# q and k products made with tokens on partitions ahead of the gMLP mixing, split and kept in DRAM with v

## The chip, the core and the metric

The kernel runs on one core of a Trainium2 chip: TensorE (PE) multiplies, VectorE (DVE), ScalarE (ACT) and GpSimd (POOL) do the rest, and SyncE (SP) issues every DMA on one queue. Times are device microseconds of one execution.

## What is computed

One layer of a decoder trunk on 1024 tokens of width 1024, all in float32:

```python
h = rmsnorm(x, norm_g)
gate_pre, a_in, a_z, b_uv, b_z, q, k, v, c_z, f_pre = split_columns(h @ w_in)
y_a = (silu(layernorm(conv31(glu(a_in)))) * silu(a_z)) @ w_a      # 512 channels
y_b = (u * (tril(w_s) @ rmsnorm(v_b) + b_s) * silu(b_z)) @ w_b    # 128-token chunks
q, k = rmsnorm(q per head), rmsnorm(k per head)                   # 8 heads of 64
s = q @ k.T / 8 + c_query - c_key, causal                         # c = cumsum(log_sigmoid(f))
y_c = ((softmax(s) @ v) * silu(c_z)) @ w_c
x = x + (sum_i sigmoid(gate_pre_i + b_gate_i) * y_i) @ w_out
```

## The kernel before

Every float32 product is made of three products of a type that TensorE takes at full rate: each operand is split into hi (rounded) and lo (the rest), and hi*hi + hi*lo + lo*hi is summed in PSUM. `h` is kept in SBUF transposed, as `h_hi` and `h_lo`, features on partitions.

Most products go through `gemm_steps` (L152): a slab of 128 weight columns is stationary, 512 tokens of `h` move, and one step of the generator is one of eight pieces of the contraction, three matmuls. A slab is 2 halves x 8 = 16 steps. `slab` (L137) loads the raw weights in two DMAs; ACT makes `w_hi` (L147), POOL `w_lo` (L148, in some stages DVE). TensorE's order is the order in which the program is written; the other engines' order is made by a scheduler with priorities. Generators wait in `queue`, and `fill(n)` (L173) issues n steps of it, so that products stand between the pieces of attention, whose data come from other engines.

The stages in order of time:

1. x is normalized and transposed, and v (with the forget gate) is made for 8 tiles of 128 tokens: `prod` (L371), tokens on partitions. v is copied to `vp` in SBUF (L391).
2. `glu_steps` (L225), four times: the conv's inputs, stored to DRAM. The conv itself is 248 taps on DVE (L265, L268), spread over the stages by `pace` (L277).
3. `mixing` (L534), 8 tiles: the gMLP's v with h stationary and 512 weight columns moving (L540, `tv`), its norm (L543, `rsqrt`), hi and lo (L547, L548) and the product with the mixing weights (L557). Steps from `queue` stand between: q and k of the first two heads (`qk_steps`, L187) and three gate products.
4. Attention, eight heads, each in ten places (L736): `turned` transposes scores (L669), `weigh` multiplies with v (L689), `score` (L624) makes a block row (products L646 and L647, bias and row minimum on DVE L650, Exp on ACT L655, scaling on POOL L658). Between them `fill` takes steps of `queue`: q and k of the next pair of heads, gate products whose raw result goes to DRAM (`gate_pre`), and the four u products.
5. The products of the z paths (`gated`), merges by branch, beside them branch A's layer norm (`norm_steps`, L842), and the output projection (L956).

q and k of a pair of heads come with features on partitions. Their mean of squares per head is a product with a matrix of blocks (`ones_hd`, L206 and L207), after which ACT, POOL and DVE normalize `qn`. For each head `ready` (L704) then calls `stack` (L597), which writes the stacked hi and lo of q and k: two casts on ACT, one on DVE, and four subtractions on POOL (L608, L611; for head 0 two of them on DVE); and `head_v` (L614), one cast on ACT and one subtraction on POOL.

Of the kernel before, what the change touches and what calls it, by code (L numbers as in the profile page):

```python
# [33 lines left out]
def trunk_kernel(ctx, tc, x, norm_g, w_in, b_gate, conv_w, conv_b, conv_norm_g, conv_norm_b,  # L34
# [152 lines left out]
    def qk_steps(c0, gcol, res):  # L187
        w = slab(w2, KC, c0)
        qn = prep.tile([P, S], F32, name="qn", bufs=2)
        res.append(qn)  # L190

        def evac(hf, ps, ts):
            raw = qn[:, ts]
            sq = prep.tile([P, HALF], F32, name="sq")
            hi = prep.tile([P, HALF], F32R, name="sqhi")
            lo = prep.tile([P, HALF], F32R, name="sqlo")
            nc.scalar.copy(raw, ps)
            nc.scalar.activation(hi, ps, AF.Square)
            nc.scalar.activation(sq, ps, AF.Square)
            nc.vector.tensor_tensor(lo, sq, f32(hi), op=ALU.subtract)  # L200

            def stat():
                y0 = prep.tile([P, HALF], F32, name="y0")
                s2 = prep.tile([P, HALF], F32, name="s2")
                st = stp.tile([P, HALF], F32, name="st", tag="st")
                nc.tensor.matmul(st, lhsT=ones_hd, rhs=hi, start=True, stop=False)  # L206
                nc.tensor.matmul(st, lhsT=ones_hd, rhs=lo, start=False, stop=True)  # L207
                rsqrt(None, st, y0, s2, s2)
                nc.gpsimd.tensor_tensor(raw, raw, y0, op=ALU.mult)
                nc.vector.scalar_tensor_tensor(raw, raw, vec[:, gcol:gcol + 1], s2,  # L210
                                               op0=ALU.mult, op1=ALU.mult)

            later.append([7, stat])

        yield from gemm_steps(w, hT, evac)


# [83 lines left out]

    with ExitStack() as ph:
# [39 lines left out]
        junk = prep.tile([P, D], F32, name="junk", tag="qn", bufs=2)  # L342
# [113 lines left out]
        qk0 = []  # L456
        queue += [glu_steps(j) for j in range(JA)]
# [556 lines left out]
```

## Time and profile before

| | us |
|---|---|
| median of 3 runs (1088.1 to 1088.93) | 1088.33 |
| the profiled execution | 1089.2 |
| its span, from the first to the last instruction | 1087.2 |
| PE busy, share of the span | 1068.3, 98% |
| DVE | 672.0, 62% |
| ACT | 472.2, 43% |
| POOL | 314.7, 29% |

Busy times are unions of the instructions' intervals. Matmuls overlap in their records, so the pace of PE is read from how many start in a stretch, not from how long one is. The granted clock is the share of full speed that TensorE was given: 1.00 is 2.4 GHz, 0.50 is 1.2 GHz.

### The profile page before, as it was taken

The numbers are of one execution on the slowest core, as the hardware profiler recorded it, in microseconds if no ns is written. First come the engines' busy times: TensorE is split into PE (matmuls) and PEld (weight loads), VectorE is DVE, ScalarE is ACT, GpSimd is POOL, SyncE is SP. The second block draws the span as 40 slices with busy tenths as digits, with TensorE's granted clock in tenths as the row PEclk, the third lists the DMA queues.
The fourth block names the chain that finished last, engine by engine and source line by source line (L and its number), as shares of the span: only waits on it lengthen the run. The fifth ranks groups of instructions, "written<-read, shape, count | busy, mean of one in ns | idle before, by whom it ended". The sixth has DMA issues, their size and how long they took to land.

```text
span 1087.2 us, 14430 instructions
## 1 busy us (share of the span) xinstructions
PE 1068.3 (98%) x5256; PEld 896.8 (82%) x5256; DVE 672.0 (62%) x1232; ACT 472.2 (43%) x885; POOL 314.7 (29%) x297
## 2 busy tenths in 40 slices
PE   8999999999999899999999999999999999999998
PEld 7988888888878788888887888878887788888887
DVE  7547788868687758885788553325653455387111
ACT  6431124424466344654574443336766433365000
POOL 0022321214665556575657554300100000000000
PEclk9999999999999899999999999999999999999999
DMA  8213321113222232133222222122345234372321
GB/s 301 82 30 99 98 68 40 30 59 104 81 59 68 76 102 67 48 99 88 59 59 86 80 87 88 39 78 65 99 137 173 70 124 127 98 244 95 107 97 58
DMA packets 109442, 99.72 MB, mean 92 GB/s; under 512 B 7405, under 2 KB 82197, under 8 KB 109372
## 3 DMA queue, kind: packets, MB, share of 16 engines
q1 hardware_dynamic: 109372, 98.81, 29.7%
q8 instruction: 41, 0.67, 0.2%
q14 instruction: 29, 0.24, 0.1%
HBM read 76.21 MB, written 22.58 MB: 91 GB/s over the span
## 4 chain that ended last, share of the span: by engine, by line
PE 78%; DVE 9%; ACT 5%; DMA 4%; issue 2%; POOL 1%; SPq 0%; DVEq 0%; ACTq 0%; POOLq 0%
PE ps L160 54%; PE ops L956 8%; PE tv L540 4%; DVE acc L268 3%; PE o L689 3%; PE tpp L669 2%; PE pa L385 1%; PE pb L386 1%; PE s L646 1%; PE s L647 1%; DMA gt<-gpre 1%; PE pm L557 1%; DVE sqlo L200 1%; DVE plo L675 1%; DMA raw<-in_w_in_dram 1%
## 5 line engine op out<-in xcount | busy, mean ns | idle before, releaser
L160 PE MATMUL ps<-h_hi,w_hi 128*128 128x512 f32 x896 | 358.1, 400 | 2.4 <-ACT w_hi L147 1.6
L160 PE MATMUL ps<-h_hi,w_lo 128*128 128x512 f32 x896 | 351.6, 392 | 4.1 <-POOL w_lo L148 3.3
L160 PE MATMUL ps<-h_lo,w_hi 128*128 128x512 f32 x896 | 350.1, 391 | 0.0
L268 DVE SCALAR_TENSOR_TENSOR acc<-a_in,cwT,acc 128x512 f32<-128x512 f32 x240 | 235.4, 981 | 3.8
L160 PEld LDWEIGHTS ps<-h_hi,w_lo 128*128 128x128 f32 x896 | 168.7, 188 | 42.7 <-POOL w_lo L148 3.8
L160 PEld LDWEIGHTS ps<-h_hi,w_hi 128*128 128x128 f32 x896 | 168.8, 188 | 33.5 <-ACT w_hi L147 3.7
L160 PEld LDWEIGHTS ps<-h_lo,w_hi 128*128 128x128 f32 x896 | 169.0, 189 | 30.1
L148 POOL TENSOR_TENSOR w_lo<-raw,w_hi 128x512 fp32r<-128x512 f32 x82 | 117.6, 1434 | 146.6 <-ACT w_hi L147 143.0
L147 ACT CAST w_hi<-raw 128x512 fp32r<-128x512 f32 x136 | 83.8, 617 | 140.2 <-PE ps L160 112.5
L160 PE MATMUL ps<-br,w_hi 128*128 128x512 f32 x384 | 118.3, 389 | 0.0
L675 DVE TENSOR_TENSOR plo<-tpp,phi 128x512 fp32r<-128x512 f32 (+1 forms) x80 | 50.6, 633 | 75.7 <-ACT phi L674 75.7
L160 PEld LDWEIGHTS ps<-br,w_hi 128*128 128x128 f32 x384 | 71.9, 188 | 14.8
L160 PE MATMUL ps<-br,w_lo 128*128 128x512 f32 x192 | 74.7, 389 | 0.0
L655 ACT ACTIVATE pt<-pt,nm 128x1024 f32<-128x1024 f32 (+3 forms) x64 | 49.7, 777 | 47.8 <-DVE nm L650 47.6
L658 POOL TENSOR_SCALAR pt<-pt,nm 128x1024 f32<-128x1024 f32 (+3 forms) x64 | 54.6, 853 | 50.6 <-DVE nm L657 50.2
L674 ACT CAST phi<-tpp 128x512 fp32r<-128x512 f32 (+1 forms) x80 | 43.5, 544 | 57.4 <-PE tpp L669 57.0
L639 POOL TENSOR_TENSOR cb<-cb,mask 128x128 f32<-128x128 f32 x64 | 43.5, 679 | 86.0 <-DVE nm L650 80.3
L148 DVE TENSOR_TENSOR w_lo<-raw,w_hi 128x512 fp32r<-128x512 f32 x54 | 38.2, 709 | 48.6 <-ACT w_hi L147 47.4
L964 DVE TENSOR_TENSOR xr<-ops,xr 128x512 f32<-128x512 f32 (+1 forms) x17 | 11.2, 660 | 72.6 <-PE ops L956 72.6
L956 PE MATMUL ops<-wo_lo,mhi 128*128 128x512 f32 (+1 forms) x136 | 51.2, 377 | 0.0
L956 PE MATMUL ops<-wo_hi,mlo 128*128 128x512 f32 (+1 forms) x136 | 51.2, 376 | 0.0
L956 PE MATMUL ops<-wo_hi,mhi 128*128 128x512 f32 (+1 forms) x136 | 51.2, 376 | 0.0
(200 smaller groups left out, 1625.4 us busy)
## 6 DMA issues: line engine op xcount, KB each, us to landing
raw<-in_w_in_dram SPq DMA_DIRECT2D x112, 256.0 KB, 2.9
gpre<-gst SPq DMA_DIRECT2D x46, 256.0 KB, 2.0
gt<-gpre SPq DMA_DIRECT2D x46, 256.0 KB, 3.0
xt<-in_x_dram SPq DMA_DIRECT2D x8, 512.0 KB, 4.1
cb<-cT_d SPq DMA_DIRECT2D x16, 256.0 KB, 3.6
wo_raw<-in_w_out_dram SPq DMA_DIRECT2D x16, 256.0 KB, 3.1
xr<-in_x_dram SPq DMA_DIRECT2D x15, 256.0 KB, 3.7
out_dram<-xr SPq DMA_DIRECT2D x15, 256.0 KB, 2.0
```

What stands on the lines that cost most here:

```text
L147: nc.scalar.copy(hi, raw)
L148: lo_eng[0].tensor_tensor(lo, raw, f32(hi), op=ALU.subtract)
L160: nc.tensor.matmul(ps, lhsT=wk[a][:, k, :], rhs=act[b][kc][:, ts], start=kc == 0 and n == 0, stop=kc == len(w) * KH - 1 and n == 2)
L268: nc.vector.scalar_tensor_tensor(acc, a_in[:, k:k + HALF], cwT[:, j, k:k + 1], acc, op0=ALU.mult, op1=ALU.add)
L540: nc.tensor.matmul(tv, lhsT=a[:, kc, ts], rhs=b[kc][:, 0:DB], start=kc == 0 and n == 0, stop=kc == KC - 1 and n == 2)
L639: nc.gpsimd.tensor_tensor(cb[:, own], cb[:, own], mask, op=ALU.add)
L655: nc.scalar.activation(pt[:, 0:kl_], pt[:, 0:kl_], AF.Exp, bias=nm[:, ci:ci + 1], scale=-1.0, accum_out=nm[:, 2:3])
L658: ins = nc.gpsimd.tensor_scalar(pt[:, 0:kl_], pt[:, 0:kl_], nm[:, 3:4], 1.0, op0=ALU.mult, op1=ALU.mult)
L674: nc.scalar.copy(phi[:, 1:n + 1], tp[:, 0:n])
L675: ins = nc.vector.tensor_tensor(plo[:, 1:n + 1], tp[:, 0:n], f32(phi[:, 1:n + 1]), op=ALU.subtract)
L689: nc.tensor.matmul(o[:, 0:2 * P], lhsT=vc[:, kb, :], rhs=part[:, src, :], start=kb == 0 and z == 0, stop=kb == 2 * g + 1 and z == 1)
L956: nc.tensor.matmul(ps, lhsT=a[kc][:, ts], rhs=b[:, kc, c:c + cols], start=kc == 0 and n == 0, stop=kc == KC - 1 and n == 2)
```

## The change

q and k are no longer made pair by pair during attention. Two new loops (`qk_tiles`) make them for all heads ahead of the mixing, in tiles of 128 tokens: h is stationary and 512 weight columns move; the mean of squares per head is a sum along the free axis; the normalized tile is transposed by four PE transposes, split into hi and lo, and stored to DRAM. v is split where it is made and stored to DRAM as hi and lo. For each head `ready` loads its six operands from there; `stack`, `head_v` and the products with `ones_hd` are gone. The `glu` slabs stand around the q and k tiles. In attention the queue now holds 23 gate products (as many as before in all) and the raw z products of six tiles (`z_pre`), which are read back by `gated_pre` in the last stages. The steps per place, the taps per place and the places of the scores are changed; there is a third PSUM buffer for scores, and three buffers instead of two for a block row.

```diff
-PLAN = (3, 2, 6, 5, 4, 3)
-GAPS = (5, 5, 5, 5, 5, 5, 5, 5, 4, 12)
-TAPS = (3, 3, 3, 3, 2, 2, 2, 2, 0, 0)
+GAPS = (5, 5, 5, 5, 5, 6, 6, 6, 5, 5)
+TAPS = (2, 2, 2, 1, 1, 1, 1, 1, 1, 1)
+NPRE = 23
+ZPRE = [(1, 0), (1, 1), (0, 0), (0, 1), (0, 2), (0, 3)]
...
+            vt = p0x.tile([P, NH, 2, HD], F32R, name="vt")
             nc.vector.tensor_tensor(fz[:, i, :], pb[:, N1:N1 + NH], bfb, op=ALU.add)
+            for n, src in enumerate((pa, pb)):
...
+                nc.scalar.copy(vt[:, hs, 0, :], src)
+                nc.vector.tensor_tensor(vt[:, hs, 1, :], src, f32(vt[:, hs, 0, :]), op=ALU.subtract)
+            nc.sync.dma_start(out=v_d[:, i, :], in_=f32(vt).rearrange("p h b d -> p (h b d)"))
...
+        def qk_tile(i, w, gcol, dst):
+            ts = slice(i * P, (i + 1) * P)
+            pq = ps0.tile([P, HALF], F32, name="pq", tag="pa", bufs=2)
+            for kc in range(KC):
+                for n, (a, b) in enumerate(((h_hi, w.hi), (h_lo, w.hi), (h_hi, w.lo))):
+                    nc.tensor.matmul(pq, lhsT=a[:, kc, ts], rhs=b[kc][:, 0:DC],
+                                     start=kc == 0 and n == 0, stop=kc == KC - 1 and n == 2)
+                if kc == KC // 2 - 1:
+                    yield
+            sq = p0x.tile([P, DC], F32, name="sq", bufs=1)
+            r = p0x.tile([P, 4, NH], F32, name="qr")
+            nc.scalar.activation(sq, pq, AF.Square, scale=float(HD) ** -0.5)
+            nc.vector.tensor_reduce(r[:, 3], sq.rearrange("p (h d) -> p h d", d=HD), axis=mybir.AxisListType.X,
+                                    op=ALU.add)
+            rsqrt(r[:, 2], r[:, 3], r[:, 0], r[:, 1], r[:, 2])
+            qn = p0x.tile([P, NH, HD], F32, name="qn")
+            nc.vector.tensor_tensor(qn, pq.rearrange("p (h d) -> p h d", d=HD),
+                                    r[:, 2].unsqueeze(2).broadcast_to([P, NH, HD]), op=ALU.mult)
+            yield
+            tp = ps0.tile([P, JC, P], F32, name="tq", tag="tp")
+            for j in range(JC):
+                nc.tensor.transpose(tp[:, j, :], qn[:, 2 * j:2 * j + 2, :].rearrange("p h d -> p (h d)"), ident)
...
+            nc.scalar.activation(hi, tp, AF.Copy, scale=gain)
+            ins = nc.vector.scalar_tensor_tensor(lo, tp, gain, f32(hi), op0=ALU.mult, op1=ALU.subtract)
+            for t, d in zip((hi, lo), dst):
+                nc.sync.dma_start(out=d[:, :, ts], in_=f32(t))
+            pace(ins, 2)
+            yield
+
+        def qk_tiles(w, gcol, dst):
+            g = [qk_tile(i, w, gcol, dst) for i in range(NT)]
+            for i in range(NT):
+                next(g[i])
+                if i > 1:
+                    next(g[i - 2])
+                next(g[i])
+            for gen in g[-2:]:
+                fill(5)
+                next(gen)
...
-        queue += [glu_steps(j) for j in range(JA)]
+        queue += [glu_steps(0)]
...
+        wq = weights(Q0)
...
+        fill(1000)
+        queue += [glu_steps(1)]
+        qk_tiles(wq, 36, qk_d[0])
+        wk = weights(K0)
...
-        queue += [qk_steps(Q0, 36, qk0), qk_steps(K0, 37, qk0)] + [gate_pre(next(gates)) for _ in range(PLAN[0])]
+        queue += [glu_steps(j) for j in range(2, JA)]
+        qk_tiles(wk, 37, qk_d[1])
+        wb = weights(BV0)
+        fill(1000)
+        queue += [gate_pre(n) for n in range(NPRE - 2)] + [z_pre(*z) for z in ZPRE]
...
+        ps_s = ph.enter_context(tc.tile_pool(name="ps_s", bufs=3, space=PSUM))
...
         def ready(h):
...
+            with tc.high_priority(offset=PRIO):
+                for t, rows_, src in ((qa, own, qk_d[0][0]), (qa, oth, qk_d[0][1]), (ka, own, qk_d[1][0]),
+                                      (ka, oth, qk_d[1][0]), (kls[e], own, qk_d[1][1])):
+                    nc.sync.dma_start(out=f32(t[rows_]), in_=src[own, p, :])
+                nc.sync.dma_start(out=f32(vc), in_=v_d[:, :, 2 * h * HD:2 * (h + 1) * HD])
...
-        fill(7)
         ready(0)
-        fill(14)
+        fill(8)
         early(score, 0, 3, 1)
-        fill(4)
+        fill(3)
         early(score, 0, 3, 0)
         fill(9)
...
+        queue += [u_slab(j) for j in range(JB)] + [gate_pre(n) for n in range(NPRE - 2, NPRE)]
-        SCORES = {0: (2, 1), 1: (2, 0), 4: (1, 1), 5: (1, 0), 6: (0, 1), 7: (0, 0), 8: (3, 1), 9: (3, 0)}
+        SCORES = {0: (2, 1), 1: (2, 0), 3: (1, 1), 4: (1, 0), 5: (0, 1), 6: (0, 0), 7: (3, 1), 8: (3, 0)}
...
-            if at == 3 and h + 1 < NH:
+            if at == 2 and h + 1 < NH:
                 ready(h + 1)
...
-    queue += [gated(bb, j, BZ0, lambda hf, ts, j=j: mixT[:, j, ts]) for j in range(2)]
     queue += [merge_steps(2, d, cc, w_c) for d in range(KC)]
...
             for _ in norm_steps(q):
                 fill(16)
+            if q < 2:
+                gated_pre(bb, 1, q, lambda hf, ts, q=q: mixT[:, q, ts])
```

## Rows read from the trace of the kernel before

**Rows 1.** The page: busy time of each engine, its share and its instructions.
```profile
PE 1068.3 (98%) x5256; PEld 896.8 (82%) x5256; DVE 672.0 (62%) x1232; ACT 472.2 (43%) x885; POOL 314.7 (29%) x297
```

**Rows 2.** Windows by stage: length, busy of PE, PEld, DVE, ACT, POOL; clock, DMA share, GB/s.
```profile
0.00:62.00 62.00, 58.69 (x440) 55.19 (x441) 39.12 (x106) 33.12 (x78) 3.40 (x11) 1.00 0.50 168
62.00:256.00 194.00, 194.00 (x900) 160.81 (x899) 146.11 (x256) 58.39 (x119) 43.43 (x32) 1.00 0.22 63
256.00:745.00 489.00, 478.87 (x2418) 403.21 (x2418) 327.78 (x605) 239.05 (x464) 262.43 (x248) 0.99 0.26 75
745.00:847.00 102.00, 99.69 (x439) 80.72 (x437) 55.35 (x106) 72.21 (x115) 5.42 (x6) 1.00 0.41 122
```

**Rows 3.** Waits of PE in attention (256 to 745 us): total, times, longest.
```profile
PE ps L160 <- POOL w_lo L148: 3.3, 1, 3.3
PE tpp L669 <- POOL pt L658: 2.2, 2, 1.5
PE st L207 <- DVE sqlo L200: 1.8, 1, 1.8
PE o L689 <- DVE oT L695: 1.3, 1, 1.3
PE ps L160 <- DVE mixT L698: 0.9, 1, 0.9
PE st L206 <- DVE s L122: 0.5, 2, 0.2
```

**Rows 4.** Timeline around the longest wait: start, duration, engine, line, operation.
```profile
349.45 3.50 POOL L608 TENSOR_TENSOR qa<-qn,qa 64x512 fp32r<-64x512 f32 x2
...
353.03 3.36 POOL L611 TENSOR_TENSOR kl<-qn,ka 64x512 fp32r<-64x512 f32 x2
...
353.90 6.34 DVE L268 SCALAR_TENSOR_TENSOR acc<-a_in,cwT,acc 128x512 f32<-128x512 f32 x3
...
359.75 0.79 PE L160 MATMUL ps<-h_hi,w_lo 128*128 128x512 f32 x1 [3.33 <-POOL w_lo L148]
```

**Rows 5.** Windows: the stretch behind that wait, clock third from the end.
```profile
359.75:365.20 5.45, 5.45 (x15) 4.48 (x16) 4.21 (x8) 1.08 (x3) 2.35 (x3) 0.50 0.37 96
```

**Rows 6.** The chain that ended last: start, duration, engine, matmuls in a piece.
```profile
88.93 65.33 PE ps L160 x288
...
239.26 5.54 PE tv L540 x24
```

**Rows 7.** Timeline: four transposes of attention, and the second matmul behind them.
```profile
417.93 0.60 PE L669 MATMUL tpp<-ident,pt 128*128 128x128 f32 x4
...
418.60 0.40 PE L160 MATMUL ps<-h_lo,w_hi 128*128 128x512 f32 x1
```

**Rows 8.** Timeline from the mixing's last product to the first loaded operand.
```profile
255.22 1.13 PE L557 MATMUL pm<-wsT,vg 128*128 128x256 f32 x8
...
256.37 2.27 SPq L632 DMA_DIRECT2D cb<-cT_d  x3
...
260.55 0.66 POOL L639 TENSOR_TENSOR cb<-cb,mask 128x128 f32<-128x128 f32 x1 [3.50 <-DMA cb<-cT_d]
```

**Rows 9.** Timeline of a mixing tile: first and last of its chain, and a tap.
```profile
232.82 0.60 ACT L543 ACTIVATE mixT<-tv 128x512 f32<-128x512 f32 x1 [4.66 <-PE tv L540]
...
235.65 0.75 DVE L548 SCALAR_TENSOR_TENSOR vg<-tv,gr,vg 128x512 fp32r<-128x512 f32 x1 [0.76 <-ACT vg L547]
236.31 0.74 DVE L268 SCALAR_TENSOR_TENSOR acc<-a_in,cwT,acc 128x512 f32<-128x512 f32 x1
```

**Rows 10.** Timeline: branch A's norm, statistics products and `nlo`, first and last quarter.
```profile
733.19 0.28 PE L866 MATMUL st<-nlo,ones_ln 128*128 128x256 f32 x1
...
738.65 0.42 DVE L862 TENSOR_TENSOR nlo<-nsum,nhi 128x256 fp32r<-128x256 f32 x1
...
801.37 0.28 PE L866 MATMUL st<-nlo,ones_ln 128*128 128x256 f32 x1
...
812.69 0.39 PE L866 MATMUL st<-nlo,ones_ln 128*128 128x256 f32 x1
```

More of the change, by code (lines that the diff above doesn't have):

```diff
@@ L184, in fill @@
                     item[1]()
[L187 to L215, printed above, removed]
     PADC = KW - 1
@@ L300, in gate_pre, with z_pre, evac @@
         yield from gemm_steps(slab(w2, KC, G0 + bi * D + d * P), hT, evac)
+    Z0 = {1: BZ0, 0: AZ0}
+    zpre = {z: dram.tile([P, S], F32, name=f"zpre{n}") for n, z in enumerate(ZPRE)}
+    def z_pre(bi, j):
+        def evac(hf, ps, ts):
+            st = prep.tile([P, HALF], F32, name="gst", bufs=2)
+            nc.scalar.copy(st, ps)
+            nc.sync.dma_start(out=zpre[bi, j][:, ts], in_=st)
+        yield from gemm_steps(slab(w2, KC, Z0[bi] + j * P), hT, evac)
     with ExitStack() as ph:
@@ L309, in trunk_kernel @@
         gb = p0.tile([P, D], F32, name="gb", tag="gbw")
+        qk_d = [[dram.tile([P, JC, S], F32, name=f"{n}{b}_d") for b in ("hi", "lo")] for n in "qk"]
+        v_d = dram.tile([P, NT, 2 * DC], F32, name="v_d")
         bfb = p0.tile([P, LINE // 4], F32, name="bfb")[:, 0:NH]
@@ L341, in trunk_kernel @@
         xts = []
-        junk = prep.tile([P, D], F32, name="junk", tag="qn", bufs=2)
+        junk = p0.tile([P, D], F32, name="junk")
         def norm(i, r, pieces):
@@ L402, in trunk_kernel @@
         with tc.high_priority(offset=8 * PRIO), tc.manual_schedule(engines=START):
-            wz = prep.tile([P, HALF], F32R, name="wz", tag="sqlo")
+            wz = p0.tile([P, HALF], F32R, name="wz")
             nc.vector.memset(f32(wz), 0.0)
@@ L479, in trunk_kernel, with weights @@
         nc.vector.tensor_copy(cwT, pc_[:, 0:JA, 0:KW])
+        def weights(c0):
+            w = Weights(c0, DC)
+            for kc in range(KC):
+                w.high(kc)
+                w.low(kc, nc.vector if kc % 3 else nc.gpsimd)
+            return w
+        wq = weights(Q0)
         lt = [p0.tile([P, NT, NH], F32, name=f"lt{n}") for n in range(4)]
@@ L581, in trunk_kernel @@
         g1 = ph.enter_context(tc.tile_pool(name="g1", bufs=1))
-        ps_s = ph.enter_context(tc.tile_pool(name="ps_s", bufs=2, space=PSUM))
+        ps_s = ph.enter_context(tc.tile_pool(name="ps_s", bufs=3, space=PSUM))
         ps_t = ph.enter_context(tc.tile_pool(name="ps_t", bufs=2, space=PSUM))
@@ L894, in trunk_kernel @@
     queue += [gated(bb, j, BZ0, lambda hf, ts, j=j: mixT[:, j, ts]) for j in range(2, JB)]
-    queue += [gated(ab, j, AZ0, norm_half(j)) for j in range(2)]
+    fill(1000)
+    for j in range(2):
+        gated_pre(ab, 0, j, norm_half(j))
     queue += [merge_steps(1, d, bb, w_b) for d in range(KC)]
-    queue += [gated(ab, j, AZ0, norm_half(j)) for j in range(2, JA)]
     fill(1000)
+    for j in range(2, JA):
+        gated_pre(ab, 0, j, norm_half(j))
     last = gate_tiles()
```

87 lines of the change are left out of this document (31 added, 56 removed).

## Prediction

> **What bounds the kernel now.** I read the page's busy times first: TensorE (PE) works 1068.3 of 1087.2 us [rows 1], so only two things can shorten the kernel: fewer or cheaper PE instructions, or less of the 18.9 us in which PE stands still. The windows by stage say where that is [rows 2]: in the first 62 us PE is idle 3.3 us, between 62 and 256 us (conv inputs, gMLP mixing) not at all, in attention (256 to 745 us) 10.1 us, in the layer norm of branch A (745 to 847 us) 2.3 us. The waits of PE in attention name the releasers [rows 3]. The longest, 3.3 us, is seen in the timeline [rows 4]: GpSimd (POOL) spends 6.9 us on the four subtractions of `stack` for head 1, a weight's `w_lo` queues behind them, and PE stands from 356 us until 359.75. After it the granted clock is 0.50 of full, the lower level, 1.2 GHz, for 5.5 us [rows 5]; half of that, 2.7 us, is what the low clock costs on top. "Busy" hides it, which is why I add it by hand. After the norm PE is idle for the remaining 3.2 us, most of it at the very end, which the change doesn't touch.
>
> A 512-column matmul lasts 0.4 us in the rows, but they overlap. The pace is read from the chain of work: 288 in 65.33 us, 0.2268 us each, and 24 of the mixing (h stationary, w moving) in 5.54 us, 0.2308 us [rows 6]. A step of a generator (three of them) is 0.68 us.
>
> **The change, part by part.** *PE work.* The q and k products stay 384 matmuls of 512 columns; the gate, z and u products are only moved. Now h is stationary, as in the mixing, whose pace is 0.004 us slower: 384 x 0.004 = +1.5 us if it is the operand order, 0 if it is the stage. I take +0.8. The 32 `ones_hd` products go: 32 x 0.2268 = -7.3 us. In their place come 2 x 8 x 4 = 64 transposes. From the first of four transposes to the second matmul behind them is 0.67 us [rows 7]; less one matmul, 0.44 us for four, 0.11 each: +7.1 us. So PE's own work changes by +0.6 us, and nothing is won there.
>
> *Attention without q/k work on the other engines.* `stack`, `head_v` and the q/k norms leave POOL, ScalarE (ACT) and VectorE (DVE); a head's operands come by DMA. Gone by construction are the `w_lo` wait 3.3 and its low clock 2.7, `sqlo` 1.8 and `st` 0.5 [rows 3, 5]: -8.3 us. The other waits (`pt` 2.2, `oT` 1.3, `mixT` 0.9, together 4.4) come from queues on POOL and DVE, which get shorter (taps per head fall from 20 to 13, too); between none and all of them I take half, -2.2. Against that the next head's first scores now have 8 steps ahead of their transposes, not 11: 2 us less lead. The nearest row is the 2.2 us of `pt` waits; with a shorter POOL queue I take +0.5, range 0 to 4.
>
> *The first head's operands.* `ready(0)` puts six loads on SP's one queue, ahead of the `cb` loads and of every slab load behind them. The space comes free when the mixing's last product ends (256.35 us); SP then issues three DMAs in 2.27 us, 0.76 each, and the first use is at 260.55, 4.2 us later [rows 8]. The score needs five of the six: 4 x 0.76 + 4.2 = 7.2 us after the release. PE has `fill(8)`, 5.4 us of work, in between. I take the difference, a stall of +1.8 us; range 0 (SP issues faster with no waits) to 9.7 (see the third rival). The Trainium skill, "DMA: Bandwidth & Descriptors", section "Anatomy of one DMA — SWDGE (gpsimd) path", fits one DMA as about 2.0 us plus its bytes over 436 GB/s, for the path that GpSimd feeds; for five loads of 262 KB run as one that is an estimate of 5.0 us, and by it the stall would be 0 and the sum -6.6 instead of -4.8. For the later heads the loads are asked for five places ahead, over 25 us; they cost nothing unless the queue stands still.
>
> *The q/k tiles.* A new stage: 16 tiles, 24 matmuls and four transposes each, 5.5 + 0.44 = 5.9 us, with no other product between them except at the ends. Two PSUM banks hold the products, so tile i+2 may start only when tile i has left its bank: Square, a sum over heads, Ln, Exp, a Newton step and the multiplication, within one tile's time. The nearest chain is the mixing's: from the Square's start (232.82) to the end of the last DVE operation (236.40) 3.6 us, with the same number of hops [rows 9]. Two conv taps per tile may stand in between, 0.74 each: 5.1 us. That fits in 5.9 us with little to spare. I take +1.0 us, from 0 to 18 (the second rival). The weight conversions for k and v lie under 32 and 64 steps of `glu`; SP's stores of hi and lo have nobody waiting before the attention.
>
> *The v tiles.* Their evacuation grows by two DVE subtractions, under 0.75 us each [rows 9], and loses copies. DVE is busy 39.1 of the first 62 us [rows 2], so 8 x 1.5 us still fit: +0.3, range 0 to 2. If DVE were the later one there, up to 2 us would show.
>
> *After attention.* The z products of six tiles come from DRAM, so 96 steps less lie there and just as many more in attention: no change of the sum. But the norm's queue holds 128 steps and wants 134: the last of eight statistics has 10 steps (6.8 us) of cover, where it had 16. Its chain took 11.3 us in the last round of before (801.37 to 812.69, PE waiting at its end) and 5.9 us in the first (733.19 to 739.07) [rows 10]. The stall is 0 to 4.5 us. ACT has fewer gated tiles to serve, which could win back up to 1 of the 2.3 us. I take +1.5, range -1 to 6.
>
> Sum: +0.8 - 7.3 + 7.1 - 8.3 - 2.2 + 0.5 + 1.8 + 1.0 + 0.3 + 1.5 = -4.8 us. It is made against the profiled span of 1087.2 us (that execution took 1089.2 us; the 2.0 us around the span stay). The median of the runs, 1088.33 us, is 0.9 us under that execution, so I forecast 1088.3 - 4.8 = 1083.5 us.
>
> **The rivals.** *All waits of attention go and nothing comes.* For it: POOL, DVE and ACT all lose work there, and no row shows a wait of PE on an ordinary slab load. Against it: the bounds above that start above nothing. -7.3 + 7.1 - 8.3 - 4.4 = -12.9: 1075.4 us.
>
> *The q/k tiles are paced by their chain, not by PE.* This is the slower side. It decides where the chain passes 5.9 us: with the 3.6 us, two taps, and the lo subtraction of an earlier tile (0.75) it is 5.8, on the edge. If DVE's order puts the taps ahead of each link, or POOL's conversions hold them up, a tile takes 6.9 us, and the 14 tiles that wait for a bank cost 14 us: -4.8 - 1.0 + 14 = +8.2, 1096.5 us. That taps can be held up is in the timeline: beside POOL's subtractions three took 6.34 us [rows 4], where one alone takes 0.74. The Trainium skill, "SBUF — State Buffer", section "SBUF: two separate sides", calls the port pair that DVE and GpSimd share an exclusive lock, held for a whole instruction; the row agrees, and by that rule one POOL conversion in a tile's chain is enough for this rival. Against it: POOL has few conversions while no `glu` steps run.
>
> *The loads come late.* SP is one queue in order. If the loads of head 0 wait behind stores, or their five transfers pass one after the other, PE stands for some 7 us and runs at the lower clock after that (2.7): -4.8 - 1.8 + 9.7 = +3.1, 1091.4 us.
>
> *The relief is not collected.* Only what goes by construction goes; the 4.4 us of other waits stay (+2.2), the shorter lead costs 2.0 (+1.5) and the short cover of the norm 2.5 (+1.0): -0.1, 1088.2 us, no change.
>
> **How the numbers follow.** Forecast 0.50, all waits gone 0.15, tiles paced by their chain 0.15, loads late 0.10, relief not collected 0.10. About 0.2%, 2.2 us, is what a measurement here can tell from no change. Faster by more than that: nine tenths of the forecast, all of the first rival, a little of the last two: 0.63. Within it: 0.16. Slower: 0.21. The range takes in the first rival and most of the way to the second: 1075 to 1095 us; the likeliest case's own range is 1079 to 1087.
>
> **What would show it.** Right: PE's waits in attention on `w_lo` and `st` are gone and its granted clock there stays at 1.00; POOL's busy time falls by a quarter; the q/k window has PE busy throughout; one wait of about 2 us before the first score, and one before the norm's last statistic. Wrong: matmuls of `pq` that wait on DVE `qn`, tile after tile (second rival); a wait of over 3 us before the first score with a clock of 0.50 behind it (third); waits on `pt` in every head (fourth).

## Result: 1118.4 us, 2.75% slower

| | before | after |
|---|---|---|
| median of 4 runs, us | 1088.55 (1088.1 to 1088.93) | 1118.4 (1116.49 to 1120.34) |
| profiled execution, us | 1089.2 | 1116.5 |
| its span, us | 1087.2 | 1114.8 |

The ratio is 1.0275, with a 95% interval of 1.0254 to 1.0296. The forecast was 1083.5 us, in a range of 1075 to 1095: wrong in sign, and outside the range. After's four runs lie at 1116.5, 1116.6, 1120.2 and 1120.3 us; the trace is of the first.

### The profile after

The page's busy times of after, beside [rows 1]:

```profile
PE 1075.2 (96%) x5288; PEld 900.3 (81%) x5288; DVE 622.9 (56%) x1252; ACT 454.3 (41%) x869; POOL 212.1 (19%) x245
```

POOL, DVE and ACT are all relieved, POOL by a third. PE, which bounds the kernel, went from 98% to 96%: its idle time grew from 18.9 to 39.6 us. The windows by stage say where (columns as in [rows 2]):

```profile
0.00:64.00 64.00, 58.61 (x436) 54.83 (x437) 40.66 (x106) 34.09 (x77) 3.17 (x11) 1.00 0.62 214
...
88.00:235.00 147.00, 140.36 (x642) 113.79 (x642) 105.14 (x177) 51.44 (x112) 19.88 (x16) 1.00 0.35 103
...
364.00:780.00 416.00, 404.31 (x2086) 342.71 (x2085) 206.50 (x482) 164.58 (x338) 151.47 (x183) 0.98 0.41 113
780.00:890.00 110.00, 100.79 (x431) 81.66 (x430) 51.16 (x97) 69.68 (x112) 11.75 (x13) 0.95 0.39 117
```

Outside the stretches shown PE is busy throughout up to 780 us. It stands still in the q/k tiles (88 to 235 us, 6.6 us), once in attention (364 to 780 us, 11.7 us) and behind attention, where branch A's norm lies (780 to 890 us, 9.2 us; its last wait comes behind 890 us). In the last two stretches the clock is below 1.00, too. The waits of PE over the span, which stand against [rows 3]:

```profile
PE s L668 <- issue: 11.7, 1, 11.7
PE st L896 <- ACT nhi L892: 8.4, 2, 5.5
PE tq L404 <- DVE qn L399: 4.6, 2, 2.4
PE ps L159 <- ACT gst L265: 2.9, 1, 2.9
PE pq L388 <- DVE qn L399: 2.0, 2, 1.2
PE tp L348 <- DVE xt L339: 1.6, 1, 1.6
```

None of the six waits of [rows 3] is left: no `w_lo` of POOL, `pt`, `oT` or `mixT`, and no `st` of the q and k statistics. Each of the new ones stands at a place that the change made.

Busy time counts a matmul at half clock as work. So I added up, from the starts of successive matmuls, by how much each gap is longer than the pace at full clock (0.228 us for 512 columns, 0.118 for 256, and so on): this takes waits and low clock together.

| lost by PE, us | before | after | change | forecast |
|---|---|---|---|---|
| h and v tiles (to 88 us) | 6.9 | 9.5 | +2.6 | +0.3 |
| q/k tiles | none there | 7.5 | +7.5 | +1.0 |
| mixing | 0 | 0 | 0 | 0 |
| first score of head 0 | in the next row | 14.2 | +14.2 | +1.8 |
| rest of attention | 15.2 | 0 | -15.2 | -10.0 |
| after attention | 4.3 | 19.9 | +15.6 | +1.5 |
| sum | 26.4 | 51.1 | +24.7 | -5.4 |

The span grew by 27.6 us; the pace of matmuls, below, has a part of the 2.9 us that the table lacks.

### The first head

The timeline of after from the end of the mixing, against [rows 8]: start, duration, engine, operation.

```profile
360.77 0.51 SPq L736 DMA_DIRECT2D kl<-klo_d  x1
...
364.22 0.33 DVE L606 SCALAR_TENSOR_TENSOR mixT<-pm,vec,bsb 128x128 f32<-128x128 f32 x1
364.58 0.45 SPq L736 DMA_DIRECT2D qa<-qhi_d  x1
...
365.73 0.59 SPq L736 DMA_DIRECT2D ka<-khi_d  x1
367.94 0.45 POOL L661 TENSOR_TENSOR cb<-cb,mask 128x128 f32<-128x128 f32 x1 [6.50 <-DMA cb<-cT_d]
368.35 1.26 POOL L147 TENSOR_TENSOR w_lo<-raw,w_hi 128x512 fp32r<-128x512 f32 x1
369.64 0.39 SPq L143 DMA_DIRECT2D raw<-in_w_in_dram  x1
370.07 0.52 SPq L736 DMA_DIRECT2D ka<-khi_d  x1
...
377.89 0.77 PE L668 MATMUL s<-ka,qa 128*128 128x512 f32 x1 [11.69 <-issue]
```

The mixing's last product ended at 360.74. The space of `qa` came free only when DVE had read `bsb` for the last time (364.55), and `qa` was issued 0.03 us later. `ka`'s second half stood on SP's queue behind a slab load, which waited for a buffer that POOL freed with a `w_lo` (369.61), itself queued behind a `cb` that waited 6.50 us for its load. From the issue of that half to the score 7.8 us went by. Then TensorE ran at the lower clock, as these windows show (the 7.8 us, the stretch behind this wait, and the one behind the longest wait in the norm):

```profile
370.07:377.89 7.82, 0.00 (x1) 0.03 (x1) 0.00 (x0) 0.00 (x0) 0.00 (x0) 0.50 1.11 211
377.89:382.60 4.71, 4.71 (x11) 3.75 (x12) 1.62 (x5) 1.68 (x3) 0.59 (x2) 0.50 1.08 221
878.14:884.30 6.16, 6.16 (x15) 4.83 (x16) 3.24 (x6) 3.44 (x5) 0.10 (x1) 0.50 0.48 140
```

### The norm

ACT and PE around the longest wait on `nhi`, against [rows 10]:

```profile
861.36 0.28 PE L896 MATMUL st<-nhi,ones_ln 128*128 128x256 f32 x1
...
869.33 1.28 ACT L837 ACT_TABLE_LOAD   x1
870.63 0.72 ACT L837 ACTIVATE gt<-gt,vec 128x512 f32<-128x512 f32 x1
871.25 0.40 ACT L885 ACTIVATE nsum<-acq 128x256 f32<-128x256 f32 x1
...
873.52 0.72 ACT L837 ACTIVATE gt<-gt,vec 128x512 f32<-128x512 f32 x1 [1.04 <-DMA gt<-gpre]
...
877.07 0.72 ACT L837 ACTIVATE gt<-gt,vec 128x512 f32<-128x512 f32 x1 [1.62 <-DMA gt<-gpre]
877.70 0.39 ACT L892 CAST nhi<-nsum 128x256 fp32r<-128x256 f32 x1
...
878.14 0.58 PE L896 MATMUL st<-nhi,ones_ln 128*128 128x256 f32 x1 [5.48 <-ACT nhi L892]
```

Between two statistics PE has 16 steps, 10.9 us; here they lie 16.8 us apart. The norm's squares share ACT with the sigmoids of the merge gates (`gt`), which wait there for their loads. In before six gated slabs (branch B's first two and branch C's four, 96 steps, no sigmoid in them) came ahead of the merges; now only branch C's four do, 64 steps, and the merges lie under the second half of the norm. Merges alone don't make the wait: in before they lie under the norm's end, four of the gates' sigmoids stand between its last two statistics, as many as here, and these are 11.3 us apart [rows 10].

### The profile page after: what moved, and what is told of

It reads as the page before. It is cut to its first block, busy times and chain, and to the rows that moved or that the text cites. A ratio compares the mean times of both kernels' runs of the same rounds, so it can differ in the third digit from the quotient of the medians.

```text
span 1114.8 us, 14701 instructions
## 1 busy us (share of the span) xinstructions
PE 1075.2 (96%) x5288; PEld 900.3 (81%) x5288; DVE 622.9 (56%) x1252; ACT 454.3 (41%) x869; POOL 212.1 (19%) x245
## 4 chain that ended last, share of the span: by engine, by line
PE 82%; DVE 6%; ACT 5%; DMA 4%; issue 3%; SPq 0%; POOL 0%; DVEq 0%; ACTq 0%; POOLq 0%
PE ps L159 50%; PE ops L992 8%; PE pq L388 6%; PE tv L584 4%; PE o L710 3%; PE tpp L690 3%; DVE acc L236 2%; PE s L668 2%; PE s L669 2%; PE pb L369 2%; PE pa L368 2%; DMA gt<-gpre 1%; DMA v_d<-vt 1%; PE pm L601 1%; ACT L837 1%
## 5 line engine op out<-in xcount | busy, mean ns | idle before, releaser
L159 PE MATMUL ps<-h_hi,w_hi 128*128 128x512 f32 x768 | 309.8, 403 | 3.6 <-ACT gst L265 2.9
L159 PE MATMUL ps<-h_hi,w_lo 128*128 128x512 f32 x768 | 302.0, 393 | 0.6 <-DVE w_lo L147 0.6
L159 PE MATMUL ps<-h_lo,w_hi 128*128 128x512 f32 x768 | 301.4, 392 | 0.0
L236 DVE SCALAR_TENSOR_TENSOR acc<-a_in,cwT,acc 128x512 f32<-128x512 f32 x240 | 197.8, 824 | 3.0
L159 PEld LDWEIGHTS ps<-h_hi,w_lo 128*128 128x128 f32 x768 | 144.9, 189 | 33.7 <-DVE w_lo L147 1.5
L159 PEld LDWEIGHTS ps<-h_hi,w_hi 128*128 128x128 f32 x768 | 145.1, 189 | 29.8 <-ACT gst L265 3.3
L159 PEld LDWEIGHTS ps<-h_lo,w_hi 128*128 128x128 f32 x768 | 145.4, 189 | 25.3
L147 POOL TENSOR_TENSOR w_lo<-raw,w_hi 128x512 fp32r<-128x512 f32 x78 | 105.0, 1346 | 210.7 <-ACT w_hi L146 209.3
L696 DVE TENSOR_TENSOR plo<-tpp,phi 128x512 fp32r<-128x512 f32 (+1 forms) x80 | 51.1, 638 | 123.0 <-ACT phi L695 123.0
L680 POOL TENSOR_SCALAR pt<-pt,nm 128x1024 f32<-128x1024 f32 (+3 forms) x64 | 47.8, 747 | 51.1 <-DVE nm L679 47.6
L388 PE MATMUL pq<-wv_hi,h_hi 128*128 128x512 f32 x128 | 51.4, 402 | 2.0 <-DVE qn L399 2.0
L672 DVE CUSTOM_DVE_ANT_0 pt<-s,cb 128x512 f32<-128x512 f32 (+1 forms) x64 | 37.6, 588 | 25.4 <-PE s L669 25.0
```

The lines of the kernel that those rows point to most:

```text
L147: lo_eng[0].tensor_tensor(lo, raw, f32(hi), op=ALU.subtract)
L159: nc.tensor.matmul(ps, lhsT=wk[a][:, k, :], rhs=act[b][kc][:, ts], start=kc == 0 and n == 0, stop=kc == len(w) * KH - 1 and n == 2)
L236: nc.vector.scalar_tensor_tensor(acc, a_in[:, k:k + HALF], cwT[:, j, k:k + 1], acc, op0=ALU.mult, op1=ALU.add)
L388: nc.tensor.matmul(pq, lhsT=a[:, kc, ts], rhs=b[kc][:, 0:DC], start=kc == 0 and n == 0, stop=kc == KC - 1 and n == 2)
L672: nc.vector.tensor_tensor_reduce(out=pt[:, c0:c0 + n], in0=s[:, 0:n], in1=cbs[h][ci][:, 0:n], scale=-float(HD) ** -0.5, scalar=nm[:, ci - ...
L680: nc.gpsimd.tensor_scalar(pt[:, 0:kl_], pt[:, 0:kl_], nm[:, 3:4], 1.0, op0=ALU.mult, op1=ALU.mult)
```

## The experiments

Each kernel is the changed one with one edit, unless it says otherwise. The kernel before ran beside each, at medians of 1086.35 to 1088.26; so I compare ratios to it. After's is 1.0275, and 0.001 is 1.1 us. Waits are those of the profiled execution, which can lie some us off the median.

| run | median, us | ratio | against after, us |
|---|---|---|---|
| e6_early | 1105.45 | 1.0158 [1.0142, 1.0173] | -12.7 |
| e11_space | 1109.36 | 1.0205 [1.0191, 1.0219] | -7.6 |
| e4_taps | 1110.18 | 1.0200 [1.0181, 1.0219] | -8.2 |
| e5_vt | 1116.22 | 1.0267 [1.0245, 1.0290] | -0.9 |
| e3_ulast | 1113.15 | 1.0238 [1.0213, 1.0262] | -4.0 |
| e8_noz | 1106.15 | 1.0170 [1.0149, 1.0190] | -11.4 |
| e2_norm | 1125.07 | 1.0348 [1.0320, 1.0377] | +7.9 |
| e7_cover16 | 1122.51 | 1.0315 [1.0289, 1.0340] | +4.4 |
| e13_table | 1117.12 | 1.0255 [1.0238, 1.0272] | -2.2 |
| e9_best | 1097.13 | 1.0090 [1.0065, 1.0115] | -20.1 |
| e10_qk | 1081.45 | 0.9946 [0.9932, 0.9959] | -35.8 |
| e12_qkz | 1095.23 | 1.0058 [1.0043, 1.0073] | -23.6 |
| e14_za | 1081.73 | 0.9940 [0.9921, 0.9958] | -36.4 |
| e15_zb | 1092.93 | 1.0045 [1.0030, 1.0060] | -25.0 |

### e6_early and e11_space: why the first head is late

e6_early gives head 0's q and k a space of their own, loaded ahead of the mixing:

```diff
+    qa0 = h0p.tile([P, S], F32R, name="qa0")
+    ka0 = h0p.tile([P, S], F32R, name="ka0")
...
+        for t, rows_, src in ((qa0, slice(0, HD), qk_d[0][0]), (qa0, slice(HD, P), qk_d[0][1]),
+                              (ka0, slice(0, HD), qk_d[1][0]), (ka0, slice(HD, P), qk_d[1][0])):
+            nc.sync.dma_start(out=f32(t[rows_]), in_=src[0:HD, 0, :])
...
+                for t, rows_, src in loads[4 if h == 0 else 0:]:
```

> The changed kernel (1118.4 us), but q and k hi/lo of head 0 have SBUF of their own and are loaded ahead of the mixing; only the lo of k and v of head 0 are still loaded at the start of attention. Theory A (time was lost at single places where PE waits; the first is the score of head 0, 11.7 us and some 2.3 us of low clock behind it): that wait is gone, 1104 to 1107 us. Theory B (DMA traffic, 120 GB/s against 92, slows the kernel all over, and a wait that is taken away comes back at the next transfer): under 4 us gained, 1114 us or more, with a new wait of PE on a load within the first head.

Measured: 1105.45 us; the wait is gone, and in attention PE lost nothing at all. So 12.7 us hung on these loads.

e11_space leaves the loads where they are and moves one pool, so that `qa` and `ka` no longer lie where `bsb` lay:

```diff
-        stk = ph.enter_context(tc.tile_pool(name="stk", bufs=2))
         pp = ph.enter_context(tc.tile_pool(name="pp", bufs=3))
         g1 = ph.enter_context(tc.tile_pool(name="g1", bufs=1))
+        stk = ph.enter_context(tc.tile_pool(name="stk", bufs=2))
```

> The changed kernel with one thing moved: the pool of the heads' operands is opened after the pools of the gates, so that the q and k operands of the first head no longer share space with the mixing's last broadcast tile, which DVE reads last. Theory A: the first head's 11.7 us wait comes mostly from space that DVE frees late; then its loads are issued at the end of the mixing or ahead of it, the wait falls to 5 us or less and the time to 1108 to 1112. Theory B: the wait is made by SP's queue (a slab load between the two halves of an operand) and by the landing of the loads; then the wait stays above 8 us and the time at 1115 or above.

Measured: 1109.36 us. SP's timeline in this kernel:

```profile
362.30 0.51 SPq L736 DMA_DIRECT2D qa<-qhi_d  x1
362.86 0.59 SPq L736 DMA_DIRECT2D qa<-qlo_d  x1
363.50 1.23 SPq L736 DMA_DIRECT2D ka<-khi_d  x2
364.77 0.59 SPq L736 DMA_DIRECT2D kl<-klo_d  x1
```

What is left of the wait (total, times, longest):

```profile
PE s L668 <- DMA kl<-klo_d: 2.6, 1, 2.6
```

The five loads now go out in one row, with no slab load in between, and 2.6 us of the wait are left. With the low clock behind it that is 4.8 us by the sum of gaps, against 14.2 in after and the forecast's +1.8. Theory A: what made the wait long was which space the tiles got, and the order of SP's queue followed from that.

### e4_taps and e5_vt: the tiles

e4_taps hands out no conv taps while the last half of the q/k tiles is made, and 17 instead of 13 in each head:

```diff
-TAPS = (2, 2, 2, 1, 1, 1, 1, 1, 1, 1)
+TAPS = (2, 2, 2, 2, 2, 2, 2, 1, 1, 1)
...
-            pace(ins, 2)
```

> The changed kernel, but the q and k tiles carry no conv taps (their 32 taps go to attention, 17 per head). Theory A (taps stand between the links of a tile's chain on DVE; waits of pq 2.0 and tq 4.6 us): those waits fall under 2 us, 1112 to 1115 us. Rival (the chain itself and the weight conversions on DVE are the cause): the waits stay over 5 us, 1117 us or more.

Measured: 1110.18 us, under Theory A's range. `tq`'s waits (4.6 us) are gone; `pq`'s 2.1 us stay (their taps come from the `glu` slabs). By the sum of gaps the q/k tiles lose 4.9 us less, and the profiled executions differ by 5.0 us. The medians differ by 8.2, with some 3 us of uncertainty either way; what the rest came from isn't shown. How the wait came about is in after's timeline of the eighth q tile:

```profile
143.27 0.68 DVE L322 TENSOR_TENSOR wv_lo<-wv,wv_hi 128x512 fp32r<-128x512 f32 x1
143.88 0.67 DVE L395 TENSOR_REDUCE qr<-sq 128x8 f32<-128x512 f32 x1
...
146.16 0.74 DVE L236 SCALAR_TENSOR_TENSOR acc<-a_in,cwT,acc 128x512 f32<-128x512 f32 x1
146.82 0.16 DVE L121 SCALAR_TENSOR_TENSOR qr<-qr 128x8 f32<-128x8 f32 x1
146.94 0.75 DVE L236 SCALAR_TENSOR_TENSOR acc<-a_in,cwT,acc 128x512 f32<-128x512 f32 x1
...
148.84 0.41 PE L404 MATMUL tq<-ident,qn 128*128 128x128 f32 x2 [2.35 <-DVE qn L399]
```

Taps stand between the links of one Newton step, 0.16 us each, and a weight conversion stands ahead of the sum. It is the second rival's mechanism, but only in the last tile of each loop, where `fill(5)` covers it, and in two tiles beside `glu` taps. The others keep pace: two tiles lie 6.02 us apart (24 matmuls in 5.57 us, then four transposes).

e5_vt gives `vt` four buffers instead of two:

```diff
-            vt = p0x.tile([P, NH, 2, HD], F32R, name="vt")
+            vt = p0x.tile([P, NH, 2, HD], F32R, name="vt", bufs=4)
```

> The changed kernel, but with four buffers for a split v tile instead of two. Theory A (ACT's copy of a v tile waits for the store of the tile two before it, 5.8 us after its issue, DVE's subtraction and the next tile's normalization behind it, and PE waits 1.6 us on xt): that wait goes, 1.5 to 2.5 us gained, 1116 us. Rival (DVE is too busy there with the two subtractions): the wait of PE on xt stays.

Measured: 1116.22 us, inside the interval of after. What speaks is the profile: the wait on `xt` (1.6 us) is gone, and PE loses 7.1 us up to 64 us, not 9.2. The trace shows a store as the cause: a `vt` was reused only when its store to DRAM had landed, 6 us after its issue.

### e8_noz and e3_ulast: the gate products that were moved

e8_noz undoes the z part alone: all z products are made in the late stages again, as in before, and attention has 42 steps a head, not 53.

```diff
-GAPS = (5, 5, 5, 5, 5, 6, 6, 6, 5, 5)
+GAPS = (4, 4, 4, 4, 4, 4, 5, 5, 4, 4)
...
-ZPRE = [(1, 0), (1, 1), (0, 0), (0, 1), (0, 2), (0, 3)]
+ZPRE = []
...
+    queue += [gated(bb, j, BZ0, lambda hf, ts, j=j: mixT[:, j, ts]) for j in range(2)]
...
-            if q < 2:
-                gated_pre(bb, 1, q, lambda hf, ts, q=q: mixT[:, q, ts])
...
```

> The changed kernel without its z part: all z products are made in the last stages again, two of them ahead of the merges of branch C, as in the kernel before; attention has 42 steps per head instead of 53. q, k and v are as in the changed kernel. Theory A (the loss after attention comes from moving the z products, and attention needs few of these steps): the waits on nhi go, those after attention fall from 20 to about 5 us; attention gains up to 4 us of waits on pt: 1102 to 1108 us. Rival (attention needs the steps): waits on pt of over 10 us there, 1112 us or more.

Measured: 1106.15 us. No wait on `nhi` is left, `gst`'s falls from 2.9 to 0.7, and behind attention PE loses some 5 us, near before's 4.3. In attention without the first score it loses under 1 us with 42 steps, where after lost nothing with 53: attention had next to no need of the z products.

e3_ulast puts the u products last in attention's queue, in place of the last two gate products, so that no raw gate waits for ACT to copy it while the merge gates begin:

```diff
-        queue += [u_slab(j) for j in range(JB)] + [gate_pre(n) for n in range(NPRE - 2, NPRE)]
+        queue += [gate_pre(n) for n in range(NPRE - 2, NPRE)] + [u_slab(j) for j in range(JB)]
```

> The changed kernel, but the four u products are the last ones in attention's queue and the two gate products stand ahead of them, as in the kernel before. Theory A (the last gate product's copy on ACT stands behind the first merge gates' sigmoids, with a table load, and holds a PSUM buffer: 2.9 us and 1.6 us of low clock): 1113 to 1115 us. Theory B: no gain, 1117 us or more.

Measured: 1113.15 us; the wait on `gst` is gone, and 1.9 us on DVE's `mixT` came in its place. That profile is of the slowest of the four, 1117.57 us, so it doesn't show what the other three gained.

### e2_norm, e7_cover16 and e13_table: what makes the norm late

e2_norm puts the last two z products of branch B ahead of the merges of branch C, so that the norm has cover without sigmoids:

```diff
+    for j in range(2):
+        gated_pre(bb, 1, j, lambda hf, ts, j=j: mixT[:, j, ts])
+    queue += [gated(bb, j, BZ0, lambda hf, ts, j=j: mixT[:, j, ts]) for j in range(2, JB)]
     queue += [merge_steps(2, d, cc, w_c) for d in range(KC)]
...
```

> The changed kernel, but the two gMLP z products that are still made at the end (tiles 2 and 3) stand ahead of the merges of branch C, as two z products stood in the kernel before, so that the norm's eight statistics meet two slabs more of plain products and fewer merges. Theory A (the merges' sigmoids, their table loads and their gate loads stand in ACT's queue ahead of the norm's squares; the two waits on nhi, 8.4 us, and the low clock behind them, some 5 us): both waits under 1 us, 1106 to 1110 us. Rival (the norm's chain is late because acc and gate loads land late on the longer DMA queue): the waits stay over 5 us in all, 1115 us or more.

Measured: 1125.07 us, a miss. Both waits on `nhi` are gone, as expected, but this came:

```profile
PE ps L159 <- ACT br L809: 12.2, 2, 11.0
```

The pool `br` has 12 buffers; the gated tiles of branch C hold eight until their merges are through, and two tiles of branch B the other four. My edit asked for more, so the products stood in PSUM until the merges had freed them. That wait lies behind the norm (926.78 us); under it the statistics are 11.1 to 11.8 us apart throughout, so with the cover back the norm kept pace. The order of before is tied to these buffers.

e7_cover16 puts the same two products behind the merges in the same queue, which gives the last statistic its 16 steps:

```diff
+    late_bb = [gated(bb, j, BZ0, lambda hf, ts, j=j: mixT[:, j, ts]) for j in range(2, JB)]
+    queue += late_bb
...
```

> The changed kernel, but the last two gMLP z products stand behind the merges of branch C in the same queue, so that the last norm statistic has 16 steps of cover instead of 10. Theory A (two waits on nhi with two causes: the last, 2.9 us, is the short cover; the one of 5.5 us had its 16 steps and is late through ACT's queue): the last wait goes, the other stays, 1113 to 1116 us. Rival (one cause, ACT's queue): both stay, 1117 us or more.

Measured: 1122.51 us, a miss in time, with a reading in its waits:

```profile
PE st L898 <- ACT nhi L894: 5.5, 2, 5.3
...
PE ps L159 <- ACT w_hi L146: 4.5, 2, 4.2
```

The last statistic's wait (2.9) fell to 0.2, the longer one stayed: there are two causes, short cover for the last one and ACT's queue for the other. The time did not follow: a wait of 4.2 us on a weight's `w_hi` came behind it. The profiled execution took 1118.13 us, and why the other three took 4.4 us more no trace shows.

e13_table asks whether ACT's changes of table make it late:

```diff
-                nc.scalar.activation(dst[hf], dst[hf], AF.Sigmoid, bias=bias)
+                nc.scalar.activation(dst[hf], dst[hf], AF.Silu, bias=bias)
```

> The changed kernel with one function exchanged: the merge gates that are read back from DRAM go through SiLU instead of the sigmoid, so ACT need not change its table between these and the norm's SiLU (the merge gates' values are changed by that; the work is the same). In the trace of the changed kernel ACT loads a table 12 times for the merge gates between 780 and 960 us, against 5 of the kernel before, 1.28 us each. Theory A: the table loads are what makes ACT reach the norm's squares late; then the waits on nhi (8.4 us together) fall below 4, that on gst (2.9) below 1.5, and the time is 1108 to 1113. Theory B: ACT is late because the merge gates stand ahead of the squares in its queue and wait there for their loads and their buffers; then fewer tables only make it wait longer for those, nhi keeps over 6 us and the time is 1114 to 1119.

Measured: 1117.12 us, not to be told from after. ACT's table loads between 780 and 960 us by line (count, busy, mean ns):

```profile
L837 ACT ACT_TABLE_LOAD x5 | 6.4, 1283 | 1.5 <-DVE w_lo L147 0.8 <-DMA gt<-gpre 0.6
L905 ACT ACT_TABLE_LOAD x1 | 1.3, 1283 | 0.0
```

And the timeline between the same two statistics:

```profile
863.40 0.28 PE L896 MATMUL st<-nhi,ones_ln 128*128 128x256 f32 x1
...
870.08 0.73 ACT L837 ACTIVATE gt<-gt,vec 128x512 f32<-128x512 f32 x1 [1.40 <-DVE part L855]
870.71 0.40 ACT L885 ACTIVATE nsum<-acq 128x256 f32<-128x256 f32 x1
...
874.35 0.72 ACT L837 ACTIVATE gt<-gt,vec 128x512 f32<-128x512 f32 x1 [2.42 <-DMA gt<-gpre]
...
877.64 0.72 ACT L837 ACTIVATE gt<-gt,vec 128x512 f32<-128x512 f32 x1 [1.36 <-DMA gt<-gpre]
...
878.71 0.39 PE L896 MATMUL st<-nhi,ones_ln 128*128 128x256 f32 x1 [4.01 <-ACT nhi L892]
```

The gates have 5 table loads instead of 12 and the norm's SiLU 1 instead of 5, so ACT is spared 14 us. Its first square starts 7.3 us behind the statistic before it (863.40 to 870.71), in after 9.9, so part of the time came through: this wait fell from 5.5 to 4.0 us. But the last one rose from 2.9 to 4.1, the two are 8.1 us together instead of 8.4, and the time stayed. Theory B, in the main: the gates ahead of the squares wait longer, for DVE to release a buffer and for their loads. The Trainium skill, "ScalarE: Activation LUTs", section "What ACT_TABLE_LOAD costs", gives one load as about 1283 ns; the rows agree to the nanosecond, yet the loads alone don't decide here.

### e9_best, e10_qk and e12_qkz: the two parts apart

e9_best has e6's, e3's and e4's edits, a third buffer for `vt`, and another set of z products made ahead (one of branch C, two of B, three of A):

```diff
-ZPRE = [(1, 0), (1, 1), (0, 0), (0, 1), (0, 2), (0, 3)]
+ZPRE = [(2, 0), (1, 2), (1, 3), (0, 1), (0, 2), (0, 3)]
...
```

> The changed kernel with all repairs: q and k of head 0 loaded early into SBUF of their own, u products last in attention's queue, no taps in the q and k tiles, three buffers for v tiles, and other z products made ahead (one of branch C, the last two of branch B, the last three of branch A), so that five plain slabs stand ahead of the merges of branch C and one behind them. Theory A (the losses add up, and what attention gained stays): 1118.4 - 13 - 5 - 8 - 2 - 13 = 1077 us, range 1072 to 1084, faster than the kernel before. Theory B (traffic): 1095 us or more.

Measured: 1097.13 us, a miss by 13 us or more. The other repairs worked, but the late stages still lost 18.7 us, with 7.1 us on `nhi` and 5.8 on `w_hi`. So I tried the parts apart. e10_qk is e8_noz (no z part) with e6's and e4's edits and a third buffer for `vt` (which the q and k tiles' hi and lo now share):

> The q, k part of the change alone, with three repairs: the z products stay where the kernel before has them (so the late stages have its cover and the attention its 42 steps a head), the first head's four operands are loaded into a space of their own ahead of the mixing, no convolution taps are handed out while the q and k tiles are made (17 a head later instead), and the v tiles have a third buffer. Theory: the tokens-first q, k path by itself is worth a gain, since it leaves the statistics products and their waits out of the attention, and all that was lost were four waits that the change brought with it; the stalls then sum to about 17 us against 26 of the kernel before, and the time is 1079 to 1085, below the kernel before. Rival: the q and k tiles' own transposes and pace cost as much as the attention gives back; then it is 1086 to 1092, no different from the kernel before or slower.

Measured: 1081.45 us, 0.5% faster than before, which the interval (up to 0.9959) sets apart from no change. Its busy times:

```profile
PE 1067.5 (99%) x5288; PEld 896.0 (83%) x5288; DVE 637.7 (59%) x1264; ACT 440.2 (41%) x851; POOL 206.5 (19%) x233
```

And its longest wait:

```profile
PE pq L391 <- DVE qn L402: 2.1, 2, 1.3
```

PE loses 17.2 us by the sum of gaps, as expected (17), against 26.4 in before. e12_qkz is e10_qk with after's z part put back:

> The q, k part alone with its repairs (1081.45 us measured), and the z products put back exactly where the changed kernel has them: six gated products ahead in the attention, 53 steps a head, and four in the late stages. Theory A: the loss of the z part lies in the late stages by itself, whatever the q and k tiles and the first head do; it is then worth again about what it was worth in the changed kernel (1118.4 - 1106.15 = 12.2 us), the waits on nhi come back at 5 to 8 us, and the time is 1090 to 1097. Theory B: the z part cost time only together with the other waits (a late attention end that the late stages inherit); then the time is 1080 to 1086.

Measured: 1095.23 us, 0.0112 of the ratio or 12.2 us more, with these waits (in an execution of 1093.01 us):

```profile
PE st L903 <- ACT nhi L899: 7.4, 2, 4.8
PE ps L159 <- ACT gst L265: 2.9, 1, 2.9
```

Theory A: the z part costs 11 to 12 us whatever else is repaired, and the waits are those of the late stages. The edits add up: e6, e4, e5 and e8 alone give -12.7 - 8.2 - 0.9 - 11.4 = -33.2 us, all four in e10_qk -35.8.

### e14_za and e15_zb: which of the z products cost

Of the six z products moved, branch A's four (64 steps) had stood behind the norm, branch B's two (32 steps) under it. e14_za is e10_qk with A's four made ahead, e15_zb with B's two:

```diff
-GAPS = (4, 4, 4, 4, 4, 4, 5, 5, 4, 4)
...
-ZPRE = []
+GAPS = (5, 5, 5, 5, 5, 5, 5, 5, 5, 5)
...
+ZPRE = [(0, 0), (0, 1), (0, 2), (0, 3)]
...
```

```diff
-GAPS = (4, 4, 4, 4, 4, 4, 5, 5, 4, 4)
+GAPS = (4, 4, 4, 5, 5, 5, 5, 5, 5, 4)
...
-ZPRE = []
+ZPRE = [(1, 0), (1, 1)]
...
-    queue += [gated(bb, j, BZ0, lambda hf, ts, j=j: mixT[:, j, ts]) for j in range(2)]
...
+            if q < 2:
+                gated_pre(bb, 1, q, lambda hf, ts, q=q: mixT[:, q, ts])
```

> The q, k part alone with its repairs (1081.45 us measured), and of the z products that the change moves only branch A's four (64 of the 96 steps) made ahead in the attention, 50 steps a head; branch B's two stay under the norm. Theory A: what costs the late stages their 12 us is that branch B's 32 steps no longer stand under branch A's norm; branch A's products come behind the norm anyway, so moving them costs nothing: no wait on nhi over 1 us, and 1080 to 1085. Theory B: any work taken out of the late stages brings their other engines' work (sigmoids, weights, loads) closer together and costs in proportion; then two thirds of 12 to 14 us come back, 1088 to 1092.

> The same with only branch B's two z products (32 of the 96 steps) made ahead, 46 steps a head, and branch A's left behind the norm. Theory A (the cover of the norm): nearly the whole loss is back, waits on nhi of 5 us or more, 1090 to 1096. Theory B (in proportion to the work taken out): a third of it, 1084 to 1087.

Measured: 1081.73 and 1092.93 us. A's 64 steps cost nothing (0.9940 against 0.9946), with no wait on `nhi`; B's 32 cost 0.0099, 10.8 us, nearly all of what the six cost together (12.2). The longest wait of e15_zb:

```profile
PE st L903 <- ACT nhi L899: 7.2, 2, 4.5
```

So the price is that of B's two products under the norm, not one for work taken out of the late stages. A rival would be that B's products, once they are read back (`gated_pre`), load ACT between the norm's quarters. No run moves that alone; against it, no SiLU of theirs stands on ACT between the two statistics of after (861.36 to 878.14), and e9_best has no `gated_pre` under the norm and waits 7.1 us. e14_za is as fast as e10_qk, and both are some 0.5% faster than before.

## Why the prediction was wrong, point by point

*Attention's relief: right, and larger.* All waits of [rows 3] went, those that I had counted by halves, too. -15.2 us against -10.0 (-8.3 - 2.2 + 0.5): my sum had low clock behind one wait only. The 2 us of shorter lead never showed.

*PE's own work: nearly right.* The q/k tiles' pace is 5.57 us for 24, 0.2321 us each. 384 x (0.2321 - 0.2268) = +2.0, where I took +0.8, and +1.5 at most: stationary h costs in this stage what it costs in the mixing, and a little more. A transpose is (6.02 - 5.57) / 4 = 0.11 us, as taken.

*The first head: the term was mis-sized, 1.8 against 14.2 us.* The third rival had the mechanism (the one queue, then the low clock) and priced it at 9.7; its sign, a wait of over 3 us before the first score and a clock of 0.50 behind it, came. The step that failed is "the space comes free when the mixing's last product ends". It came free at the last read of a tile that happened to lie there, 3.8 us later, and while the loads waited for it, a slab load got ahead of one of them. The 4.2 us from issue to use were short, too: the last half took 7.8 us, with the DMA engines full. e11_space shows that without the late space the term would have been 2.6 us of waiting, 4.8 with the low clock.

*The q/k tiles: the term was mis-sized, +1.0 against +7.5; e4_taps took 4.9 us of it away.* The second rival's mechanism (taps between the links on DVE), in four tiles and not in fourteen. The chain fitted in the other twelve. The step that failed is "Two conv taps per tile": in the first tile of each loop five taps of the `glu` slabs stood between its sum and its last multiplication (98.27 to 102.08 us), and in the last tile a weight conversion and two taps, more than `fill(5)` covers.

*The v tiles: mis-sized, +0.3 against +2.6.* I costed DVE's subtractions and left out that the store holds the buffer.

*After attention: the step that failed outright, +1.5 against +15.6.* "No change of the sum" counted PE steps alone. But 32 of the 96 moved steps had been the cover of branch A's norm (e15_zb: 10.8 us). Without these two gated slabs the merges begin two statistics earlier, and each of them brings sigmoids to ACT that wait for loads. I saw the short cover of the last statistic (2.9 us, inside my 0 to 4.5) and not the longer wait ahead of it. No rival of mine had this place.

With attention's -15.2 against a sum of +39.9 at the other places, the table's +24.7 is accounted for. The experiments confirm the sizes of the first head (12.7 of 14.2) and of the late stages (11.4 of 15.6), and two thirds of the q/k tiles' (4.9 of 7.5); the pace (2.0 us) is worked out from rows alone. Left open is why e9_best, which kept branch B's two products under the norm and took one of branch C's away (16 steps), lost as much: its wait on `nhi` fits the cover, but no run took that one alone. Nor is it settled which wait sets the squares' delay on ACT, the gates' loads or DVE's release of their buffers; e13_table shows both, and that the table loads alone don't set it; and why four gates cost 5.5 us there and next to nothing between the last two statistics of before isn't shown.

## What to carry to other kernels

Work that fills gaps has two addresses. Before moving it, list who stands behind it at the place it leaves: here 32 of 96 steps were taken from over a chain on ACT, at 10.8 us, and the place they went to needed none. When operands come by DMA into space that another stage used, ask which tile lay there and which engine reads it last: here the loads began only then, 3.8 us late, and an unrelated load stood on the queue between two halves of one operand. A space of its own for the first use was worth 12.7 us. And split a change into its parts early: the part with q and k was +18.5 us as it stood (e8_noz, 1.0170) and -5.9 us with its repairs (e10_qk, 0.9946), and the change with both parts +29.9.

## What the runs showed of the hardware

The page's median for `ka` is 6.4 us from issue to landing in after, where a slab load of the same 256 KB takes 3.1 us there; in e10_qk it is 5.3 and 2.8. I had taken 4.2 from [rows 8]. The DMA share of 1.11 in the window from 370.07 us (`ka`'s second half under way) and of 1.08 in the one behind it (1.00 is all 16 engines busy) shows them full there: the second head's loads were issued right behind the first's (from 371.27 us). The Trainium skill, "DMA: Bandwidth & Descriptors", section "Anatomy of one DMA — SWDGE (gpsimd) path", by which the five loads were estimated at 5.0 us, is for another issuing path, and no run here measured five loads alone; in e11_space they took from 362.30 to about 370 us.
